# One more block of the up projection with seven products for eight, and other places for the plain units

## The chip, the cores and the metric

The kernel runs on one core of a Trainium2 chip. The metric is the device time of one execution in microseconds. The kernel before takes 1564.11 us (median of three runs, 1563.72 to 1564.22).

## What is computed

One encoder block on 256 tokens (SEQ) of width 2048 (D_MODEL), all in float32: a retention branch and an attention branch, merged by gates, and then an MLP with squared ReLU. The change touches the MLP alone:

```python
z = _rmsnorm(h, norm_mlp_g[l]) @ w_up[l]          # (256, 2048) @ (2048, 8192)
h = h + jnp.square(jax.nn.relu(z)) @ w_down[l]    # (256, 8192) @ (8192, 2048)
return _rmsnorm(h, norm_f_g)
```

## The kernel before

**Number format.** Every float32 operand is split in two parts of the type fp32r: `hi` is the rounded value, made by a cast on ScalarE, and `lo` is the rest, made by a subtraction on VectorE (`split`, L548 to L551). A product is then three matmuls: hi by hi, hi by lo, lo by hi. So each weight tile costs a cast, a subtraction and three passes of TensorE, and VectorE and ScalarE work on weights throughout.

**Two ways through the up projection.** The 8192 columns of `w_up` are computed in two ways.

- A *unit* (`class Unit`, L1264) computes 128 columns for all 256 tokens, with the weights standing in TensorE. It has two parts, one for each half of the depth 2048. A part loads 512 KB, makes one split of 128x1024, and runs eight matmuls of 512 columns (`t_pass1`, L176) and eight of 256 (`t_pass2`, L180). After the second part `evict` (L1288) copies the bank on ScalarE (L1291), adds its halves on VectorE (L1292), and two parts later ScalarE does relu (L1295) and square (L1256), and GpSimd's queue stores the result to a buffer `hid` in HBM (L1257).
- A *block* computes 1024 columns in eight *steps* (`class Step`, L287; `SJ` is 8), with the seven-product form of a 2x2 matrix product: combinations of the operands are made first, then seven products stand for eight. A step covers 256 of the depth and 1024 columns. Its weights come in two loads of 512 KB (`sraw`, L300, and `raw`, L301). VectorE makes the weight forms (L307 for `fa`, L316 and L317 for `fb`). The step has four parts: part 0 takes the raw tile `ra` and makes two products, part 1 takes `fa` and makes two, part 2 takes `fb` and makes two, part 3 takes the remaining raw half-tile and makes one. Each product is three matmuls (L333 to L335). The seven products gather over the eight steps in seven PSUM banks: 3, 4, 2 and 5 in the pool `pmm`, 6, 1 and 7 in the pool `pat`, which has four banks. Units and turns use `pat` too, and so share its last bank while a block runs.

After a block's last part `s_end` (L515) combines the seven banks: four copies on ScalarE and four operations on VectorE at once, and three more on VectorE some parts later (`SUMS`). The result lies with tokens on partitions, and four *turns* (L1302) transpose it on TensorE, four transposes of 128x128 each (L1309), into a bank of `pat`; ScalarE applies relu (L1261) and square and the result is stored. The turns of a block run in part 1 of steps 1 to 4 of the next block, ahead of that part's products; those of the last block run behind the last two units.

**Operand combinations.** The activation side of a block needs combinations too (`Combos`, `combine`, L221 to L245): eight pairs, made two at a time. Two of the four groups are made while the first block runs, started by part number (`MAKE`: at parts 7 and 24) and advanced at even part numbers, four stages of VectorE and ScalarE work each. They borrow two of the five `raw` buffers.

**The order of work.** `stream` (L470) goes through a list `parts`, in which the order is written out: for each part n it issues the loads up to six parts ahead, the splits up to `AHEAD` = 4 parts ahead, and then the matmuls of part n with whatever hangs on it (an eviction, a block's end, a turn). All engines keep this program order. So an eviction of part n stands in ScalarE's and VectorE's queues ahead of the splits of part n + 5.

**How the list is built** (L1331 to L1354). The first three units come ahead (first halves, then second halves), the last two at the end. Before the change `SU` is 3: three blocks compute 3072 columns, and the other 5120 columns are 40 units. Of these, 35 stand between the parts of the steps: one after part 3 of every step but the last of all (23), and twelve more after part 1 of steps 0, 2, 4 and 6 of each block. Behind the last unit the down projection follows in the same list, starting with the hidden pairs that the units made and ending with those of the blocks (`order`, which begins at `ST // 2`).

Of the kernel before, what the change touches and what calls it, by code (L numbers as in the profile page):

```python
# [27 lines left out]
CHUNK = 64  # L28
DFF = 8192
FT = DFF // P  # L30
SU = 3
SJ = KT // 2
ST = SU * 1024 // P
EARLY, LATE = 3, 2
AHEAD = 4
PAIRED = 6
MAKE = 7, 2 * EARLY + 18
SUMS = (4, 7, 10), (0, 1, 2)
MANUAL = {getattr(mybir.EngineType, n) for n in ('Activation', 'DVE', 'PE', 'SP', 'Pool')}
# [66 lines left out]
def block_kernel(ctx: ExitStack, tc: tile.TileContext, A):  # L106
# [1195 lines left out]
    def turn(u, jj):  # L1302
        pT = atps(f"zt{u}{jj}")
        for j in range(2):
            kt = 2 * jj + j
            for t in range(2):
                o = j * S + t * P
                src = zo[:, 0, 2 * t + kt // 4, kt % 4 * P : kt % 4 * P + P]
                PE.transpose(pT[:, o : o + P], src, ident)  # L1309
        square(4 * u + jj, pT)  # L1310

    def step(u, j, qs):
        def end():
            sums = s_end(qs, zo[:, 0].rearrange("p (t c) n -> p t c n", t=2), zo[:, 1])
            next(sums)
            later.extend([d, lambda: next(sums)] for d in SUMS[u == SU - 1])
            turns.extend(lambda jj=jj: turn(u, jj) for jj in range(4))
# [13 lines left out]
    early = [Unit(i, 0) for i in range(EARLY)]  # L1331
    parts = [(e, h) for h in range(2) for e in early]
    units = list(range(EARLY, FT - ST - LATE))
    slots = [(u, j, h) for u in range(SU) for j in range(SJ) for h in (1, 3)][:-1]
    whole = [t for t in slots if t[2] == 3]
    room = len(units) - len(whole)
    halves = [t for t in slots if t[2] == 1]
    if room >= 0:
        use = set(whole) | {halves[i * len(halves) // room] for i in range(room)}
    else:  # L1340
        use = {t for t in whole if t[1] != PAIRED or t[0] >= -room}
    for u in range(SU):
        qs = {}
        for j in range(SJ):
# [69 lines left out]
    def finish(half, t, c, n, lo=0, hi=512):  # L1414
        h = residual(half, t, c)[:, lo:hi]
        ps = both[half].q[ROLE[t, c]][:, lo:hi]
        V.scalar_tensor_tensor(h, in0=ps, scalar=rh2[:, t : t + 1], in1=h, op0=ALU.mult, op1=ALU.add)

        def square():
            SC.activation(ps, h, AF.Square, accum_out=ssf[:, t, n : n + 1])  # L1420

        return square
# [90 lines left out]
    with tc.manual_schedule(engines=MANUAL):  # L1513
        stream(parts, after)
        assert not later
        for t in range(2):
            for c in range(2):
# [10 lines left out]
                else:  # L1528
                    halves = [finish(1, t, 1, 3, 0, 256)]
# [86 lines left out]
```

## Time and profile before

| what | us |
|---|---|
| median of three runs | 1564.11 |
| the profiled execution | 1564.87 |
| its span, first to last instruction | 1563.1 |
| busy: TensorE matmul / weight load | 1550.3 / 1310.8 |
| busy: VectorE / ScalarE / GpSimd | 1317.3 / 962.8 / 39.1 |
| up projection, first unit to first matmul of the down projection | 344.48 |

PE stands for TensorE's matmuls, PEld for its weight loads, DVE for VectorE, ACT for ScalarE, POOL for GpSimd and SP for the engine that issues the weight loads. A row of a timeline begins with the start in us from the start of the span and the duration in us; then come engine, line, operation, output and input, shape, and the count of like instructions in a row; a bracket tells the idle time ahead of it and what ended it. Matmul durations overlap, so that the cost of one is the distance between starts. A row of the waits is: who waited for whom, us in total, times, longest. Names are those of the tiles in the code without their numbers: `zs` is a block's bank, `z` a unit's, `zt` a turn's, `zo` the combined result of a block, `hs` a result on its way to `hid`, `hc` and `hT` the operands, `dn` the down projection's bank.

### The profile page before, as it was taken

Reading aid. Unit: us, or ns where it says so; the run is one execution under the profiler, and the core shown is the slowest. Engines: PE = TensorE matmul, PEld = TensorE weight load, DVE = VectorE, ACT = ScalarE, POOL = GpSimd, SP = SyncE. Lnnn points to the kernel's source line nnn. Section 1 sums busy time; section 2 is a strip of 40 time slices with the busy share of each in tenths; the row PEclk is TensorE's granted clock in tenths of the full one; section 3 lists DMA queues with packets and bytes.
Section 4 is the critical chain, followed back from the end, with each engine's and each line's share of the span. In section 5 each row is a group of like instructions: output and inputs, shape, how many; then the busy total and the mean of one; then the engine's idle time right before and its main releaser. Section 6 shows DMA issues by size and latency. Waiting matters only on the chain.

```text
span 1563.1 us, 21388 instructions
## 1 busy us (share of the span) xinstructions
PE 1550.3 (99%) x7655; PEld 1310.8 (84%) x7655; DVE 1317.3 (84%) x1787; ACT 962.8 (62%) x1416; POOL 39.1 (3%) x76
## 2 busy tenths in 40 slices
PE   9999999999999999999999999999999999999997
PEld 7888888888898888888888888888888888888886
DVE  7998877899977988976566698887978899989996
ACT  7546555566545667874445566676767766656664
POOL 0000000000000000000000000000000100000000
PEclk9999999999999999999999999999999999999999
DMA  8666755466656664445556657676675977686773
GB/s 328 208 202 208 234 163 160 154 202 211 203 170 222 207 197 149 158 127 164 191 197 217 234 193 252 210 229 229 212 247 190 375 269 240 235 308 210 265 256 115
DMA packets 107626, 333.70 MB, mean 213 GB/s; under 512 B 11264, under 2 KB 12160, under 8 KB 106496
## 3 DMA queue, kind: packets, MB, share of 16 engines
q1 hardware_dynamic: 104208, 318.71, 61.3%
q0 software_dynamic: 3168, 11.54, 1.8%
q10 hardware_dynamic: 144, 2.10, 0.4%
q8 instruction: 60, 0.98, 0.2%
q14 instruction: 46, 0.38, 0.1%
HBM read 319.72 MB, written 12.58 MB: 213 GB/s over the span
## 4 chain that ended last, share of the span: by engine, by line
PE 78%; DVE 2%; issue 1%; ACT 1%; DMA 0%; DVEq 0%; POOLq 0%; POOL 0%; ACTq 0%
PE z L176 9%; PE dn L359 7%; PE dn L358 7%; PE dn L357 7%; PE z L180 5%; PE zs L335 2%; PE zs L333 2%; PE zs L334 2%; PE mo L214 2%; PE mo L215 2%; PE mo L217 2%; PE wo L214 2%; PE wo L215 2%; PE wo L217 2%; PE gm L357 2%; PE yr L358 2%
## 5 line engine op out<-in xcount | busy, mean ns | idle before, releaser
L169 DVE TENSOR_TENSOR lo<-raw,hi 128x1024 fp32r<-128x1024 f32 (+1 forms) x148 | 173.2, 1172 | 90.9 <-ACT hi L168 90.8
L551 DVE TENSOR_TENSOR lo<-raw,hi 128x1024 fp32r<-128x1024 f32 (+3 forms) x214 | 232.1, 1101 | 20.1 <-ACT hi L550 19.6
L168 ACT CAST hi<-raw 128x1024 fp32r<-128x1024 f32 (+1 forms) x148 | 149.6, 1012 | 156.0 <-PE mo L215 44.9
L550 ACT CAST hi<-raw 128x1024 fp32r<-128x1024 f32 (+3 forms) x214 | 199.9, 953 | 51.6 <-issue 7.9
L551 DVE TENSOR_TENSOR morelo<-raw,morehi 128x1024 fp32r<-128x1024 f32 (+1 forms) x118 | 127.1, 1098 | 19.0 <-ACT morehi L550 18.5
L550 ACT CAST morehi<-raw 128x1024 fp32r<-128x1024 f32 (+1 forms) x118 | 109.1, 949 | 10.7 <-PE dn L359 2.9
L550 ACT CAST hi<-forms 128x1024 fp32r<-128x1024 f32 x70 | 73.7, 1052 | 51.8 <-DVE forms L307 26.3
L176 PE MATMUL z<-hT,morehi 128*128 128x512 f32 x408 | 101.6, 391 | 0.0
L357 PE MATMUL dn<-hi,dd 128*128 128x512 f32 x230 | 89.6, 389 | 0.0
L359 PE MATMUL dn<-hi,dd 128*128 128x512 f32 x230 | 89.5, 389 | 0.0
L358 PE MATMUL dn<-lo,dd 128*128 128x512 f32 x230 | 89.5, 389 | 0.0
L551 DVE TENSOR_TENSOR lo<-forms,hi 128x1024 fp32r<-128x1024 f32 x70 | 85.0, 1220 | 5.3 <-ACT hi L550 4.9
L176 PEld LDWEIGHTS z<-hT,morehi 128*128 128x128 f32 x408 | 74.9, 188 | 14.4
L1291 ACT COPY hs<-z 128x512 f32<-128x512 f32 x40 | 23.5, 587 | 70.6 <-PE z L180 70.6
L357 PE MATMUL dn<-morehi,dd 128*128 128x512 f32 x156 | 60.7, 389 | 0.0
L358 PE MATMUL dn<-morelo,dd 128*128 128x512 f32 x156 | 60.7, 389 | 0.0
L359 PE MATMUL dn<-morehi,dd 128*128 128x512 f32 x156 | 60.7, 389 | 0.0
L180 PEld LDWEIGHTS z<-hT,morelo 128*128 128x128 f32 x408 | 55.6, 190 | 4.0
L176 PE MATMUL z<-hT,hi 128*128 128x512 f32 x232 | 57.9, 392 | 0.0
L307 DVE TENSOR_TENSOR forms<-raw,sraw 128x1024 f32<-128x1024 f32 x46 | 56.1, 1219 | 1.1 <-DMA raw<-w_up_s 1.1
L180 PE MATMUL z<-hT,morelo 128*128 128x256 f32 x408 | 56.9, 282 | 0.0
L358 PEld LDWEIGHTS dn<-lo,dd 128*128 128x128 f32 x230 | 43.2, 188 | 9.0
(500 smaller groups left out, 4195.1 us busy)
## 6 DMA issues: line engine op xcount, KB each, us to landing
raw<-w_down SPq DMA_DIRECT2D x106, 512.0 KB, 6.1
raw<-w_up SPq DMA_DIRECT2D x80, 512.0 KB, 4.9
raw<-w_rv SPq DMA_DIRECT2D x32, 512.0 KB, 4.9
raw<-w_rg SPq DMA_DIRECT2D x32, 512.0 KB, 4.0
raw<-w_gret SPq DMA_DIRECT2D x32, 512.0 KB, 4.4
raw<-w_ret_o SPq DMA_DIRECT2D x32, 512.0 KB, 5.0
raw<-w_gmla SPq DMA_DIRECT2D x32, 512.0 KB, 4.3
raw<-w_mla_o SPq DMA_DIRECT2D x32, 512.0 KB, 3.7
```

The lines of the kernel that those rows point to most:

```text
L168: SC.copy(hi, raw)
L169: V.tensor_tensor(out=lo, in0=raw, in1=hi.bitcast(F32), op=ALU.subtract)
L176: PE.matmul(out, w[0][:, k], x.both(k0 + k), start=start and k == 0, stop=False)
L180: PE.matmul(out[:, :S], w[1][:, k], x.hi(k0 + k), start=False, stop=stop and k == n - 1)
L214: PE.matmul(out, x.hi(k0 + k, ts), w[0][:, k], start=start and k == 0, stop=False)
L215: PE.matmul(out, x.lo(k0 + k, ts), w[0][:, k], start=False, stop=False)
L217: PE.matmul(out, x.hi(k0 + k, ts), w[1][:, k], start=False, stop=stop and k == nk - 1)
L357: PE.matmul(q, ah, wh, start=start, stop=False)
L358: PE.matmul(q, ah, wl, start=False, stop=False)
L359: PE.matmul(q, al, wh, start=False, stop=self.left[f] == 0)
L550: SC.copy(hi, val)
L551: V.tensor_tensor(out=lo, in0=val, in1=hi.bitcast(F32), op=ALU.subtract)
```

## The change

`SU` becomes 4: four blocks compute 4096 columns, 32 units the other 4096. With three units ahead and two at the end, 27 stand among the steps. Their places are written down anew: one after part 1 of each step but steps 0 and 4 of a block (`WHOLE`), and one after part 3 of a block's last step, between that block and the next. `PAIRED` and the general rule go. The weights are laid out to match, since `_s_steps` and `_t_units` take their columns by `SU`, and `ST`, the count of 128-column groups in blocks, goes from 24 to 32, so that the hidden pairs of the units are 16 to 31 and those of the blocks 0 to 15.

```diff
-SU = 3
+SU = 4
...
-PAIRED = 6
+WHOLE = 0, 4
...
     units = list(range(EARLY, FT - ST - LATE))
-    slots = [(u, j, h) for u in range(SU) for j in range(SJ) for h in (1, 3)][:-1]
-    whole = [t for t in slots if t[2] == 3]
-    room = len(units) - len(whole)
-    halves = [t for t in slots if t[2] == 1]
-    if room >= 0:
-        use = set(whole) | {halves[i * len(halves) // room] for i in range(room)}
-    else:
-        use = {t for t in whole if t[1] != PAIRED or t[0] >= -room}
+    use = {(u, j, 1) for u in range(SU) for j in range(SJ) if j not in WHOLE} | {(u, SJ - 1, 3) for u in range(SU - 1)}
     for u in range(SU):
```

`MAKE`, `SUMS`, `AHEAD`, the first three units and the last two stay as they are.

## The prediction

> **What bounds the kernel now.** I read the page first, then the table of busy time by stretches, the waits of the up-projection stage, and the timelines of single steps in it. The columns of the table are length, busy time (instructions) of PE, PEld, DVE, ACT and POOL, granted clock, DMA share and GB/s. Its first row is the whole up projection (first unit matmul to first matmul of the down projection), then two pairs of steps, then the down projection.
>
> ```profile
> span 1563.1 us, 21388 instructions
> PE 1550.3 (99%) x7655; PEld 1310.8 (84%) x7655; DVE 1317.3 (84%) x1787; ACT 962.8 (62%) x1416; POOL 39.1 (3%) x76
> ```
> ```profile
> 876.13:1220.61 344.48, 344.41 (x1841) 296.85 (x1840) 290.75 (x332) 236.12 (x338) 26.12 (x48) 1.00 0.67 225
> 962.62:988.90 26.28, 26.28 (x140) 22.63 (x139) 21.31 (x24) 16.69 (x23) 1.62 (x3) 1.00 0.63 216
> 1015.18:1042.43 27.25, 27.25 (x149) 23.43 (x147) 22.46 (x26) 18.82 (x27) 2.70 (x5) 1.00 0.68 227
> 1220.61:1520.00 299.39, 299.39 (x1324) 247.89 (x1323) 285.87 (x345) 193.44 (x246) 3.22 (x6) 1.00 0.78 270
> ```
> ```profile
> PEld zs L335 <- DVE lo L551: 0.5, 1, 0.5
> DVE hs L1292 <- ACT hs L1291: 26.7, 19, 2.8
> ```
> TensorE is full, at a granted clock of 1.00, and in the whole up projection it waits once, 0.5 us, for a split on VectorE. So the stage lasts as long as its matmuls, and 344.48 us is their sum. But VectorE is busy 290.75 of these 344.48 us (84%), and it cannot use all of the rest: the queue is in order, and 26.7 us go into standing at a unit's eviction until ScalarE has copied the bank.
>
> What TensorE pays for a step and for a unit stands in its timeline:
>
> ```profile
> 909.68 0.40 PE L333 MATMUL zs<-hi,hT 128*128 128x512 f32 x1
> ...
> 914.47 1.98 PE L176 MATMUL z<-hT,morehi 128*128 128x512 f32 x8
> ...
> 920.03 0.40 PE L333 MATMUL zs<-morehi,hT 128*128 128x512 f32 x1
> ```
> Durations overlap, so I take starts. A step (21 matmuls) is 914.47 - 909.68 = 4.79 us, 0.228 per matmul: its parts 0, 1, 2 have six (1.37 us), part 3 has three (0.68). A unit is 920.03 - 914.47 = 5.56. As a check, two steps and three units are 26.26, and the row has 26.28. The pair with two turns in it is 27.25, so a turn is 0.97 / 2 = 0.485.
>
> VectorE's side of a step, of a block's end and of a unit's eviction:
>
> ```profile
> 1035.96 1.22 DVE L307 TENSOR_TENSOR forms<-raw,sraw 128x1024 f32<-128x1024 f32 x1
> 1037.10 1.22 DVE L551 TENSOR_TENSOR lo<-sraw,hi 128x1024 fp32r<-128x1024 f32 x1
> 1038.24 0.68 DVE L316 TENSOR_TENSOR forms<-forms,sraw 128x512 f32<-128x512 f32 x1
> 1038.95 0.69 DVE L317 TENSOR_TENSOR forms<-forms,raw 128x512 f32<-128x512 f32 x1
> 1039.56 2.42 DVE L551 TENSOR_TENSOR lo<-forms,hi 128x1024 fp32r<-128x1024 f32 x2
> 1041.90 0.69 DVE L551 TENSOR_TENSOR lo<-raw,hi 128x512 fp32r<-128x512 f32 x1
> ```
> ```profile
> 997.69 2.14 DVE L520 TENSOR_TENSOR zo<-zs,zo 128x512 f32<-128x512 f32 x3
> 999.74 0.68 DVE L520 TENSOR_TENSOR zo<-zo 128x512 f32<-128x512 f32 x1
> 1000.34 1.22 DVE L551 TENSOR_TENSOR lo<-raw,hi 128x1024 fp32r<-128x1024 f32 x1
> ```
> ```profile
> 894.60 0.42 DVE L1292 TENSOR_TENSOR hs<-hs 128x256 f32<-128x256 f32 x1
> ```
> By starts again: part 0 of a step is 3.60 us (1.14 + 1.14 + 0.71 + 0.61), parts 1 and 2 are 1.17 each, part 3 is 0.60 (the spacing of the 128x512 rows at 999.74 and 1000.34). **A step is 6.54 us on VectorE against 4.79 on TensorE.** A unit is two splits of 1.14 and 0.34 for its add: 2.62 against 5.56. The units are what lets VectorE keep up. A block's end is 2.65 at once and three more of 0.60 later: 4.45.
>
> **What the change removes and adds.** Eight units go and a block of eight steps comes. The count is what the words say: 64 - 32 - 5 = 27 units stand among the steps, and 6 x 4 + 3 = 27. On TensorE that is -8 x 5.56 + 8 x 4.79 + 4 turns x 0.485 = **-4.2 us**, and the old wait of 0.5 has no reason to return in its place: -0.5. On VectorE it is 8 x 6.54 + 4.45 - 8 x 2.62 = +35.8: busy 326.6 in a stage whose matmuls now need 340.3, 96%. So on average it still fits, and the question is where it does not fit locally. The bytes stay the same (a step and a unit both load 1 MB), and ScalarE stays below VectorE. The down projection takes its hidden pairs in another order, but the same shapes and positions; I cost it at nothing, covered by stores that are many steps old; a pair that came late would show as a wait for its load.
>
> *Block 0.* Before, a unit follows step 0's part 1 and another its part 3; now step 0 has none, and the first unit stands in step 1. Besides its steps VectorE makes two groups of operand combinations there, placed by part number (parts 8 to 14 and 24 to 30), and this place does not move, so the second one now falls onto step 3's unit and step 4, which has no unit:
>
> ```profile
> L231 DVE TENSOR_TENSOR raw<-hT x2: 1218/1218/1219, 900.4 to 933.1; 128x1024 f32<-128x1024 f32 x2
> L237 DVE TENSOR_TENSOR raw<-raw x2: 418/418/419, 906.8 to 936.5; 128x256 f32<-128x256 f32 x2
> L238 DVE TENSOR_TENSOR raw<-raw x2: 418/419/420, 907.2 to 936.8; 128x256 f32<-128x256 f32 x2
> L240 DVE TENSOR_TENSOR raw<-raw,raw x2: 418/418/418, 909.8 to 939.2; 128x256 f32<-128x256 f32 x2
> L241 DVE TENSOR_TENSOR raw<-raw,raw x2: 425/426/426, 910.2 to 939.7; 128x256 f32<-128x256 f32 x2
> L551 DVE TENSOR_TENSOR hc<-raw,hc x2: 1216/1216/1216, 912.6 to 946.0; 128x1024 fp32r<-128x1024 f32 x2
> ```
> ```profile
> 893.75 0.40 PE L333 MATMUL zs<-morehi,hT 128*128 128x512 f32 x1
> ```
> A group is 4.13 us of durations, 3.65 less 0.08 of overlap each. From the last early unit's add (894.60 + 0.34 = 894.94, a time that the change leaves alone) VectorE has, up to the split that part 1 of step 5 needs: four steps 26.16, three units 7.86, parts 0 and 1 of step 5 4.77, the combinations without the last split 3.65 + 2.51. That is 44.95 us, done at 939.9 if it never waits. TensorE starts step 0 at 893.75, step 1 at 898.54, and wants that split 4 steps, 3 units, one part and two matmuls later: 898.54 + 19.16 + 16.68 + 1.37 + 0.46 = 936.2. VectorE is 3.7 us late, and about 0.3 for signals and weight loads that show: **+4.0** (my bounds are 3 and 6). The upper bound is for a load that comes late:
>
> ```profile
> raw<-w_up_s SPq DMA_DIRECT2D x23, 512.0 KB, 4.4
> ```
> Step 2's second load goes out when the split of step 1's unit frees its buffer, at 894.94 + 3.60 + 1.17 + 1.14 = 900.9, and lands at about 905.3; VectorE gets to it at 905.6 (a step, two unit splits and 1.8 of combinations after 894.94). Two us later would be two us more. After step 5 every step has its unit, and per step and unit VectorE needs 9.16 of 10.35, so it recovers.
>
> *Between blocks.* A block ends: unit of step 7, its parts 2 and 3, one unit, then step 0 and parts 0 and 1 of step 1 without any unit. Splits are issued four parts ahead, behind the unit's eviction in the queue. At the end of step 7's unit (call it 0) the queue has nothing further done than the next unit's splits. The add ends at about 1.15 (0.15 for the signal, estimated; copy and add). Then VectorE does step 0 6.54, the block's end 2.65, the next unit's add 0.34, and parts 0 and 1 of step 1 3.60 + 1.17: done at 15.45. TensorE wants it at 2.05 + 5.56 + 4.79 + 1.37 + 0.485 + 0.46 = 14.71. With 0.15 for the signal: 0.9 late.
>
> The second wait there is new in kind. Each turn (one in part 1 of steps 1 to 4 of the next block) writes a bank of a pool of four, of which three hold products 6, 1 and 7; the unit right behind part 1 needs the same last bank, and has to wait until ScalarE's relu has read the turn. ScalarE's rows:
>
> ```profile
> 1026.22 0.59 ACT L1291 COPY hs<-z 128x512 f32<-128x512 f32 x1 [2.65 <-PE z L180]
> 1026.71 1.05 ACT L550 CAST hi<-forms 128x1024 fp32r<-128x1024 f32 x1
> 1027.65 0.62 ACT L550 CAST morehi<-raw 128x512 fp32r<-128x512 f32 x1
> 1028.17 0.60 ACT L1261 ACTIVATE hs<-zt 128x512 f32<-128x512 f32 x1
> 1028.81 0.63 ACT L1256 ACTIVATE hs<-hs 128x512 f32<-128x512 f32 x1
> 1029.35 0.40 ACT L1295 ACTIVATE hs<-hs 128x256 f32<-128x256 f32 x1
> 1029.78 0.42 ACT L1256 ACTIVATE hs<-hs 128x256 f32<-128x256 f32 x1
> 1030.10 1.03 ACT L550 CAST morehi<-raw 128x1024 fp32r<-128x1024 f32 x1
> ```
> By starts: a big cast 0.94, a small one 0.52, the relu of a turn 0.60, the last two operations of a unit 0.75. This is a turn with a unit behind it, and only two casts lie between the copy and the relu; the pair of 27.25 us shows no wait. In the new order the queue holds more. In step 1 the forms are ready at 11.82 (1.15 + 6.54 + 2.65 + 0.34 + 1.14), then come a cast, a unit's end, three casts, a small cast and the relu: 0.94 + 0.75 + 2.82 + 0.52 + 0.60 = 5.63, with the signal 17.6; TensorE is there at 14.25 + 1.37 + 0.9 = 16.5: 1.1 to 1.2 more. In steps 2 and 3, from the end of the unit before: 0.15 + 0.49 + two casts 1.88 + 0.75 + 0.94 + 0.52 + 0.60 + 0.15 = 5.5 against 2.05 + 1.37 + 0.485 + 1.37 = 5.27: 0.25 each (bounds 0 and 0.6). Together 0.9 + 1.2 + 0.5 = 2.6 at each of three boundaries: **+7.8** (bounds 4 and 11).
>
> The Trainium skill (Perfetto Trace Analysis, the section on matmuls under tensor performance) advises that independent matmul groups rotate through different PSUM banks, so that one group's evacuation runs beside the next one's matmuls. That speaks against the new places; taken alone it would price the nine pairs of turn and unit at a whole evacuation each, 9 x 0.60 = 5.4 us, where the queue's order gives 3 x 1.7 = 5.1. The pair of 27.25 us, in which the bank is shared too, shows that sharing alone costs nothing.
>
> At step 4, where a turn but no unit stands, the same sums leave 0.9 us of slack (the split of step 5's part 1 at 8.25 after the unit of step 3, wanted at 9.15), so I cost it at nothing in blocks 1 to 3. If VectorE still lagged there, its lag would show.
>
> **Sum.** -4.2 - 0.5 + 4.0 + 7.8 = +7.1 us. The profiled execution took 1564.87 (span 1563.1 and 1.8 around it, which stays), so it would be 1572.0; the median of the runs, 1564.11, is 0.76 below that one, so I forecast **1571.2 us**. A check from the other side: VectorE's 326.6 us and its old 26.7 us at evictions are 353.3 for the stage, +8.8.
>
> **Rivals.** *All of it is covered* (the other side). The down projection runs VectorE at 285.87 of 299.39 us (95%) without a TensorE wait. If the up stage did so at 96%, only -4.7 would be left: 1559.4. Its place is the start of a block; it decides if step 1's forms are done by about 9.7 instead of 11.8 after the last unit, earlier by both waits (0.9 and 1.2), which brings the relu forward as well. Against it: the down parts are even, while a unit's eviction holds back the queue here. [...] I give 0.12.
>
> *Only VectorE's lag counts*, and the bank is handed back in time: -4.7 + 4.0 + 2.7 = +2.0, 1566.1, no measurable change. For it: the waits in steps 2 and 3 are within the error of the sum; against it: the 1.2 us in step 1 is not. 0.18.
>
> *VectorE never recovers*: if it also keeps a wait of 1.4 us (26.7 / 19) at each of 32 evictions, the stage is 326.6 + 44.8 = 371.4, +26.9, 1591.0. Against it: waiting for a copy is what a late queue stops doing. 0.08.
>
> **How the numbers follow.** The forecast itself has 0.62, with a range of its own of 1566.4 to 1576.4 (the two sums at their bounds are 7 to 17, against -4.7, on 1564.11). Two runs of this kernel can be told apart at about 0.2%, 3.1 us. Faster by more than that is only the first rival, 0.12; within it, the second, 0.18; slower, the forecast and the last, 0.70. The range of 1563.5 to 1578 leaves out the first and the last rival.
>
> **What would show it.** In the changed profile the stage should take about 351.5 us instead of 344.48, DVE about 327 busy in it. TensorE should wait for lo in steps 2 and 5 of block 0, and near the end of part 1 of step 1 of blocks 1, 2 and 3; z should wait for the relu of the turn (L1261) behind it. Per pair of step and unit elsewhere 10.35, with a turn 10.84 to 11.1. I am wrong if the stage is under 345 us, if TensorE's waits are for DMA, or if the down projection's 299.39 us move by more than 1.

## The result, and the profile after

The change takes 1571.62 us (median of four runs, 1571.23 to 1572.55), the kernel before 1564.16 beside it (1563.72 to 1564.43): 1.0049 times as long, 95% interval 1.0031 to 1.0066. It is slower by 7.5 us, more than the 0.2% that a measurement can tell. A later repeat (e11) gave 1571.65 against 1564.58, ratio 1.0046 (1.0033 to 1.0059). The profiled execution took 1572.55 us, where the prediction's sum gave 1572.0 for it. Its page begins:

```profile
span 1570.8 us, 21306 instructions
PE 1551.3 (99%) x7583; PEld 1303.9 (83%) x7583; DVE 1349.0 (86%) x1826; ACT 970.2 (62%) x1420; POOL 37.0 (2%) x72
```

72 matmuls fewer, and yet a longer span. The busy table by stretches, with the columns as in the prediction, shows where: the whole up projection, one pair of step and unit inside a block, and the same 1324 matmuls of the down projection as before.

```profile
876.58:1228.30 351.72, 344.63 (x1770) 289.30 (x1768) 322.70 (x371) 243.40 (x342) 23.98 (x44) 1.00 0.66 220
1033.76:1044.11 10.35, 10.35 (x55) 8.86 (x53) 9.31 (x11) 6.68 (x10) 0.54 (x1) 1.00 0.67 212
1228.30:1527.69 299.39, 299.39 (x1324) 247.90 (x1323) 285.77 (x345) 193.39 (x246) 3.24 (x6) 1.00 0.77 270
```

The stage went from 344.48 to 351.72, +7.24; the down projection is the same to the hundredth; a pair inside a block costs 10.35 as before, and the clock is 1.00 in all three. So the loss lies in the stage and at certain places in it. The waits of the stage, for weight loads and then for VectorE's evictions:

```profile
PEld z L176 <- ACT hs L1261: 6.8, 9, 1.3
PEld zs L335 <- DVE morelo L551: 4.7, 4, 2.0
PEld zs L335 <- DVE lo L551: 3.4, 5, 0.9
```
```profile
DVE hs L1292 <- ACT hs L1291: 15.1, 14, 2.6
```

Before, TensorE had one wait of 0.5 here. Now it has nine for the relu of a turn and nine for a split. The timeline of the weight loads tells where (the bracket is the idle time of the loads; some of it hides behind matmuls under way):

```profile
911.81 0.19 PEld L335 LDWEIGHTS zs<-lo,hc 128*128 128x128 f32 x1 [0.92 <-DVE lo L551]
...
937.25 0.19 PEld L335 LDWEIGHTS zs<-morelo,hT 128*128 128x128 f32 x1 [1.47 <-DVE morelo L551]
...
940.50 0.19 PEld L335 LDWEIGHTS zs<-morelo,hc 128*128 128x128 f32 x1 [2.03 <-DVE morelo L551]
...
985.38 1.69 PEld L176 LDWEIGHTS z<-hT,hi 128*128 128x128 f32 x8 [1.34 <-ACT hs L1261]
...
996.54 1.67 PEld L176 LDWEIGHTS z<-hT,hi 128*128 128x128 f32 x8 [0.47 <-ACT hs L1261]
```

The first three lie in block 0, in part 1 of step 2 and in parts 0 and 1 of step 5. The other two stand at the first boundary: the unit behind part 1 of step 1 of block 1, and the unit of step 2. A like one follows in step 3 (0.45), and two waits for splits, 0.42 and 0.80, come ahead of them in step 1; all five come again at the two later boundaries.

What they cost is read from the starts of the matmuls:

```profile
928.76 0.40 PE L333 MATMUL zs<-morehi,hc 128*128 128x512 f32 x1
...
941.54 0.63 PE L176 MATMUL z<-hT,morehi 128*128 128x512 f32 x2
...
980.44 0.39 PE L334 MATMUL zs<-hi,hT 128*128 128x512 f32 x1
...
981.16 0.40 PE L333 MATMUL zs<-hi,hc 128*128 128x512 f32 x1
...
982.52 0.40 PE L334 MATMUL zs<-hi,hc 128*128 128x512 f32 x1
983.28 0.50 PE L335 MATMUL zs<-lo,hc 128*128 128x512 f32 x1 [0.36 <-DVE lo L551]
983.62 0.39 PE L333 MATMUL zs<-hi,hc 128*128 128x512 f32 x1
...
984.09 0.40 PE L335 MATMUL zs<-lo,hc 128*128 128x512 f32 x1
985.39 2.12 PE L176 MATMUL z<-hT,hi 128*128 128x512 f32 x8 [0.91 <-ACT hs L1261]
```

From 928.76 to 941.54 stand 42 matmuls of steps (parts 2 and 3 of step 3, step 4, parts 0 and 1 of step 5): 12.78 us for 42 x 0.228 = 9.58. That is 3.20 lost; 0.78 more is lost at 911.81, where the 21 matmuls between two units take 5.57 for 4.79. Block 0 loses **3.98**. At the boundary a matmul of a step follows the one before by 0.228 where nothing waits. From 980.44 to 981.16 it is two in 0.72, 0.26 lost; from 982.52 to 983.62 two in 1.10, 0.64 lost: **0.9** for the two splits. From 984.09 to the unit's first it is 1.30, 1.07 lost, and a unit behind such a wait takes 5.67 to 5.71 for 5.56: **1.2** for the bank in step 1. In steps 2 and 3 the unit's first comes 0.42 after the matmul before it, 0.19 lost, and with the slower unit it is 0.31 and 0.33. A boundary loses 2.75, the three **8.3**. Together that is 12.3. In e10 below, where TensorE waits nowhere, the same number of matmuls makes a stage of 339.42, and 351.72 is 12.30 more.

### The profile page after: what moved, and what is told of

Same layout as the page of the kernel before. It is cut to its first block, busy times and chain, and to the rows that moved or that the text cites. A ratio compares the mean times of both kernels' runs of the same rounds, so it can differ in the third digit from the quotient of the medians.

```text
span 1570.8 us, 21306 instructions
## 1 busy us (share of the span) xinstructions
PE 1551.3 (99%) x7583; PEld 1303.9 (83%) x7583; DVE 1349.0 (86%) x1826; ACT 970.2 (62%) x1420; POOL 37.0 (2%) x72
## 4 chain that ended last, share of the span: by engine, by line
PE 73%; DVE 4%; ACT 2%; issue 2%; DMA 0%; DVEq 0%; POOLq 0%; POOL 0%; ACTq 0%
PE dn L358 7%; PE dn L359 7%; PE dn L357 7%; PE z L176 6%; PE z L180 3%; PE zs L335 2%; PE zs L333 2%; PE zs L334 2%; PE mo L214 2%; PE mo L215 2%; PE mo L217 2%; PE wo L217 2%; PE wo L214 2%; PE wo L215 2%; PE gm L359 2%; PE gm L357 2%
## 5 line engine op out<-in xcount | busy, mean ns | idle before, releaser
L551 DVE TENSOR_TENSOR lo<-raw,hi 128x1024 fp32r<-128x1024 f32 (+3 forms) x236 | 251.6, 1082 | 26.6 <-ACT hi L550 25.6
L550 ACT CAST hi<-raw 128x1024 fp32r<-128x1024 f32 (+3 forms) x236 | 217.1, 938 | 57.4 <-issue 9.4
L551 DVE TENSOR_TENSOR morelo<-raw,morehi 128x1024 fp32r<-128x1024 f32 (+1 forms) x88 | 93.8, 1084 | 2.9 <-ACT morehi L550 2.8
L550 ACT CAST morehi<-raw 128x1024 fp32r<-128x1024 f32 (+1 forms) x88 | 81.1, 941 | 7.0 <-issue 2.1
L550 ACT CAST morehi<-forms 128x1024 fp32r<-128x1024 f32 x51 | 53.6, 1050 | 44.9 <-DVE forms L307 26.2
L551 DVE TENSOR_TENSOR lo<-forms,hi 128x1024 fp32r<-128x1024 f32 x57 | 69.5, 1220 | 3.2 <-ACT hi L550 2.5
L176 PEld LDWEIGHTS z<-hT,hi 128*128 128x128 f32 x288 | 52.3, 188 | 14.4 <-ACT hs L1261 4.5
L551 DVE TENSOR_TENSOR morelo<-forms,morehi 128x1024 fp32r<-128x1024 f32 x51 | 62.2, 1219 | 2.2 <-ACT morehi L550 1.7
L176 PE MATMUL z<-hT,morehi 128*128 128x512 f32 x224 | 56.2, 393 | 0.9 <-ACT hs L1261 0.9
L357 PEld LDWEIGHTS dn<-hi,dd 128*128 128x128 f32 x240 | 45.0, 188 | 9.4
```

Of the source, the lines that this page charges most:

```text
L176: PE.matmul(out, w[0][:, k], x.both(k0 + k), start=start and k == 0, stop=False)
L357: PE.matmul(q, ah, wh, start=start, stop=False)
L550: SC.copy(hi, val)
L551: V.tensor_tensor(out=lo, in0=val, in1=hi.bitcast(F32), op=ALU.subtract)
```

## The experiments

The theory was the prediction's: the order costs three separate sums. VectorE is behind in block 0, through the early steps without units and the combinations; it is behind again where a block's end meets steps without units; and ScalarE's queue gives a turn's bank back late. The main rival was that the fourth block itself is too much, wherever its units stand. Every length called "stage" runs from the first unit matmul to the first matmul of the down projection in the profiled execution. The times of each kernel before beside the experiments are 1564.4 (e1 to e4), 1564.6 (e5 to e8), 1564.6 (e9 to e11) and 1564.6 (e12).

**e1: is it the turn's bank?** The turn moves from part 1 of the step, right ahead of the unit, to part 3, behind it.

```diff
-            if part == 1:
+            if part == 3:
                 self.between()
```

> The changed kernel, but each turn stands ahead of part 3 of its step instead of part 1, so that 3.4 us of matmuls lie between a turn and the next unit. Theory (the unit behind a turn waits for the one free bank of the pool, 9 waits, 1.2 us in step 1 and 0.25 in steps 2 and 3, after ScalarE's relu in its queue): the nine waits for L1261 vanish; without the turn's 0.485 us ahead of it, part 1 of step 1 waits somewhat longer for VectorE, 1.4 instead of 0.9; a boundary loses 1.4 instead of 2.6 us, so 3.6 less in all: 1568.0 us. Rival (VectorE is the bound, and the bank's wait only covers what VectorE would cost anyway): the waits move to VectorE's lo, and the time stays at 1571 to 1572.

Measured 1568.39 us, ratio 1.0024 (1.0015 to 1.0033), stage 347.96: 3.8 of the 7.2 us come back. Its waits in the stage:

```profile
PEld zs L335 <- DVE morelo L551: 5.3, 4, 2.0
PEld zs L335 <- DVE lo L551: 4.2, 5, 1.2
PEld zt L1309 <- ACT hs L1291: 0.7, 3, 0.2
```

The relu's nine waits are gone, and the waits for splits are a little longer, since TensorE now comes to them earlier. The bank's share is real and separable.

**e2: is it where the combinations fall?** The second group starts eight parts earlier.

```diff
-MAKE = 7, 2 * EARLY + 18
+MAKE = 7, 2 * EARLY + 10
```

> The changed kernel with the second group of operand combinations begun at part 16 instead of part 24, that is beside steps 2 and 3 of block 0 and no longer beside step 4, which has no unit. Theory (VectorE's queue from 894.9 us on has 45 us of work up to part 1 of step 5, wherever the combinations stand in it): block 0 still loses 4.0 us, spread otherwise, 1571.6 us within 1. Rival (the loss comes from the combinations falling onto the step without a unit): block 0 loses 1.5 us, 1569.

Measured 1572.83, ratio 1.0053 (1.0041 to 1.0066), stage 352.84. The waits of block 0 now come in six pieces instead of three, in part earlier. So it is not the place of the group that counts but its amount of work: VectorE has no pause in this stretch into which it could be moved.

**e3: do the splits come too late?** While blocks run, the splits of a part are issued five parts ahead in place of four, so that VectorE's spare time inside a block is used ahead of the boundary.

```diff
-    def stream(parts, after):
+    def stream(parts, after, deep=0):
...
-            while prepped < min(len(parts), n + ahead + 1):
+            while prepped < min(len(parts), n + ahead + 1 + (0 < n < deep)):
...
     assert not units
+    deep = len(parts)
...
-        stream(parts, after)
+        stream(parts, after, deep)
```

> The changed kernel with the splits of the up projection issued five parts ahead instead of four; nothing else moves. Theory (at a block's end VectorE's queue stands idle behind the eviction of step 7's unit, with nothing issued beyond the next unit's splits): part 0 of the next block's first step gets done in that idle time, VectorE is then 2 to 3 us early at step 1, the wait for lo there (0.9 us) and the relu's lateness in step 1 (1.2) go, the 0.25 in steps 2 and 3 stay, block 0 loses about 0.7 less: 1564.6 us. Rival (VectorE has too much to do over the stage as a whole): look-ahead makes no work less, at most 2 us come back, 1569.6 or more.

Measured 1567.16, ratio 1.0016 (1.0007 to 1.0025), stage 347.03: 4.7 us come back, less than expected.

```profile
PEld z L176 <- ACT hs L1261: 5.9, 9, 1.6
PEld zs L335 <- DVE morelo L551: 3.3, 3, 1.6
PEld zs L335 <- DVE lo L551: 0.2, 1, 0.2
```

No boundary has a wait for a split any more, and those of block 0 fell from 4.4 (0.92 + 1.47 + 2.03) to 3.5; but the bank's waits stay. I had taken it that the earlier forms would bring the relu forward. They do, but one more split is issued ahead of it, and so one more cast stands in ScalarE's queue before it.

**e4 and e5: is it the places, or the fourth block?** e4 is four blocks under the old rule for the units (one after part 3 of every step but step 6); e5, set up when the result of e4 was known, leaves out step 3 in place of 6. Both bring back the lines of the old rule that the diff removes, with

```diff
-WHOLE = 0, 4
+PAIRED = 6
```

in e4 and `PAIRED = 3` in e5.

> Four blocks, but the units in the places of the rule of before: after part 3 of every step except step 6 (and the last). So the block count alone, without the new places. Theory (the places make the waits, not the count): no wait for L1261, since two parts lie between a turn and the next unit; block 0 loses nearly nothing, since its steps 0 to 5 all have a unit; at each boundary the block's end is late in VectorE's queue, behind the splits of steps 6 and 7, and product 4 of the next block waits about 1.2 us for its bank: -4.7 + 3.7, 1563 us (1560 to 1566). Rival (with four blocks VectorE is 96% busy, and that costs wherever the units stand): 1569 or more.

> Four blocks with the units after part 3 of every step except step 3 (and the last): the kernel with the old places, but the pair of steps without a unit between them moved from 6 and 7, at the block's end, to 3 and 4. Theory (a block's end must not meet a late VectorE): a unit now stands after step 6, so that step 7 starts with its splits done; the waits at the three boundaries (0.6 us for lo in step 0, 1.1 us of the turn for the unit's copy, 0.5 for the bank of product 4) go, 4 to 5 us; block 0 keeps the 2.4 us in step 2 that a late load cost (raw of step 2 came 1.5 us after VectorE was ready for it), plus 0.6 where the second group of combinations falls onto steps 3 and 4: 1563 us (1561 to 1565). Rival (VectorE at 96% costs some 3 us over matmuls wherever the gap is): 1568 or more, as with the old places.

Measured: e4 1568.94, ratio 1.0027 (1.0017 to 1.0038), stage 347.53; e5 1568.45, ratio 1.0027 (1.0017 to 1.0038), stage 348.51. Both expectations failed. The waits of e4, TensorE's and then one of VectorE's:

```profile
PEld zs L335 <- DVE morelo L551: 5.0, 5, 2.4
PEld zt L1309 <- ACT hs L1291: 3.4, 3, 1.1
```
```profile
DVE forms L307 <- DMA raw<-w_up_s: 1.5, 1, 1.5
```

The relu's waits are absent, as expected, and at the boundaries a turn waits for a unit's copy instead. In e5, where they were expected to vanish, these shrink to 1.3 us in three waits. But block 0 loses time under each of the three orders: by the starts of its matmuls 3.98 us in the change, 3.2 in e4 (weight loads wait 2.38 and 1.13) and 8.3 in e5 (1.91, 2.15, 0.91 and 2.38). In e4 and e5 loads of `raw` arrive late as well (waits of 1.5 and 2.9 us); that this is because the combinations hold two of the five buffers is the reading that e7 tests. So the rival has a part of the truth. With the places of before, too, the fourth block would have cost more than it saves, 3.1 us by the stage and 4.5 by the medians; the change's own places cost another 3 to 4.

Of e5's 8.3 us, 1.6 are no wait. Behind the wait of 2.38 eight matmuls of steps start 0.43 apart instead of 0.228, from 948.31 to 951.71, and the granted clock of this stretch is 0.50. In e7 below the same happens behind waits of 1.31 and 1.94, from 955.43 to 958.83, again at 0.50. Why the clock falls there, and not behind the waits of the change, no run here shows.

**e6: both repairs.** e1 and e3 together, on the change's places.

> The changed kernel with both: turns ahead of part 3 of their steps, and splits of the up projection five parts ahead. Theory (bank wait and eviction wait are separate terms and add up): the boundaries lose nothing any more, block 0 its 3.3 us as with the deeper look-ahead alone, 1563 us (1562 to 1564.5). Rival (both cures free the same time): no better than the better of the two, 1567.

Measured 1562.95, ratio 0.9991 (0.9982 to 1.0), stage 342.68. All the boundaries are clean but for one 0.5 us wait of a turn; what stays is block 0's 3.5 us of waits. Each repair alone gave 3.2 to 4.5 us of run time, both give 8.7: with the turn behind the unit, the cast that e3 puts ahead of the relu no longer holds up a weight load.

**e7: e5 with the combinations later.**

```diff
-MAKE = 7, 2 * EARLY + 18
+MAKE = 11, 2 * EARLY + 26
```

> As the kernel with the pair of steps at 3 and 4, and the two groups of operand combinations begun at parts 11 and 32 instead of 7 and 24, so that the load of step 2 goes out before the first group takes two of the five raw buffers, and the second group stands behind the pair of steps. Theory: the 2.4 us in step 2 and the 0.6 at steps 3 and 4 go, and some 1 us stays: 1560.5 us (1559.4, all covered, to 1562). Rival (block 0's loss is VectorE's work, not the load): as without the move, 1563.

Measured 1566.33, ratio 1.0012 (1.0003 to 1.0021), stage 346.59. It is 2.1 us below e5 and far above the 1562 at most that the theory gave, and above its rival too.

```profile
PEld zs L335 <- DVE lo L551: 2.0, 2, 1.2
PEld zs L334 <- DVE hc L551: 1.9, 1, 1.9
PEld zs L333 <- ACT hc L550: 1.3, 1, 1.3
```

No load is late now, which fits the buffers as the reason for that. But the products wait for the combinations themselves (`hc`), which are needed by their own step, and 1.6 us go with the lower clock. Made earlier, the combinations make the splits late; made later, they are late themselves.

**e8 and e10: is that all?** The two late groups of combinations are left out of the change (e8) and of e6 (e10).

```diff
-MAKE = 7, 2 * EARLY + 18
+MAKE = ()
...
-            o = self.t[j // 4][:, j % 4]
+            o = self.t[0][:, j % 4]
```

> The changed kernel without the two groups of operand combinations in block 0: the products of steps 4 to 7 of each block use the combinations of steps 0 to 3 instead, so that part of the computation is left out; every matmul, load and split of weights stays. Theory (VectorE's queue up to part 1 of step 5 decides block 0): 6.2 us less of VectorE's work make it 2.5 us early instead of 3.7 late, block 0 loses nothing, the boundaries keep their 8: 4.0 less, 1567.6 us. Rival (steps 0 and 4 without units starve TensorE by themselves): 2 us or more of the loss stay, 1569.6 or more.

> The kernel with turns ahead of part 3 and splits five parts ahead, without the two groups of operand combinations (the products of steps 4 to 7 use those of steps 0 to 3, so that part of the computation is left out). Theory (three terms, block 0, VectorE's lag and the bank at the boundaries, are all of the loss): nothing is left of it, and the matmuls alone decide: 4.7 us below the kernel before, 1559.6 on the scale of 1564.4. Rival (something else costs too): 1561 or more.

Measured: e8 1567.83, ratio 1.0021 (1.0013 to 1.003), stage 347.63; e10 1559.89, ratio 0.997 (0.9958 to 0.9982), stage 339.42. In e8 the waits are those of the boundaries alone:

```profile
PEld z L176 <- ACT hs L1261: 6.8, 9, 1.3
PEld zs L335 <- DVE lo L551: 2.4, 4, 0.8
PEld zs L335 <- DVE morelo L551: 1.2, 2, 0.8
```

The 6.8 for the relu is the figure of the change; the two others are (0.42 + 0.80) x 3. So block 0 loses its 4.1 us only with the combinations, the steps without units do not starve TensorE by themselves, and the two places do not act on each other. In e10 TensorE waits nowhere in the stage: the three terms are the whole of the loss.

**e9: the combinations on GpSimd**, which is idle 98% of the time, in e6.

```diff
-        V.tensor_tensor(out=a2, in0=a11, in1=a12, op=ALU.subtract)
+        E.tensor_tensor(out=a2, in0=a11, in1=a12, op=ALU.subtract)
...
-            return combine(self.pair, 2 * c, self.t[-1][:, c % 2 * 2 : c % 2 * 2 + 2])
+            return combine(self.pair, 2 * c, self.t[-1][:, c % 2 * 2 : c % 2 * 2 + 2], E=G if c > 1 else V)
```

> The kernel with turns ahead of part 3 and splits five parts ahead, and besides the additions and subtractions of the two groups of operand combinations in block 0 on GpSimd, which is busy 2% of the time; their splits stay on ScalarE and VectorE. Theory (what is left of the loss, 3.3 us in block 0, is VectorE's 45 us of work up to step 5): VectorE sheds 5.0 us there, no wait for lo stays in block 0: 1559.7 us (1559 to 1560.5). Rival (GpSimd's operations, whose length no run here has shown, come too late for the splits behind them, or slow VectorE): the splits wait in order, 1563 or more.

Measured 1567.17, ratio 1.0016 (1.0007 to 1.0025), stage 346.95, 4.3 more than e6. The rival held; its lines are in the last section.

**e12: a unit where block 0 lacks one.** e6, with the one unit that the last block can spare given to step 4 of block 0.

```diff
-WHOLE = 0, 4
+WHOLE = (0,), (0, 4), (0, 4), (0, 4, 6)
...
-if j not in WHOLE
+if j not in WHOLE[u]
```

> The kernel with turns ahead of part 3 and splits five parts ahead, and one unit moved: step 4 of block 0 gets one, step 6 of block 3 loses its own (both after part 1). Theory (the rest of the loss is VectorE's queue up to step 5 of block 0, 3.3 us): the unit gives TensorE 5.56 us there for 2.62 of VectorE's, 2.9 us of slack, and block 3, where VectorE has caught up and no combinations are made, has room for a second pair of steps without a unit: block 0 loses 0.4, block 3 nothing to 1, so 1560.5 us (1559.5 to 1561.5) against 1564.4 before. Rival (the unit taken away is missed where it stood): the loss moves to block 3, 1563.

Measured 1560.16, ratio 0.9973 (0.9962 to 0.9983), its stage and its waits (columns as above):

```profile
875.45:1215.19 339.74, 339.74 (x1769) 290.46 (x1768) 322.28 (x371) 243.32 (x342) 24.04 (x44) 1.00 0.68 228
```
```profile
PEld zs L335 <- DVE lo L551: 0.5, 2, 0.3
PEld zt L1309 <- ACT hs L1291: 0.2, 1, 0.2
```

339.74 is what the prediction's sum for the matmuls alone gives, 344.48 - 4.2 - 0.5 = 339.8; that it is so close is partly chance, since e10 has 339.42 without any wait. Of block 0's waits 0.5 us at two weight loads is left, though the combinations are made as before: what is lost there takes both, the combinations and a step without a unit. And nothing is lost in block 3 where the unit was taken away. The kernel does all the work of the change, with four blocks, and is 4.4 us faster than the kernel before and 11.5 faster than the change. The fourth block's saving is there; three decisions about order had spent it.

## Why the prediction was right, step by step

**The matmuls, -4.2, and the old wait, -0.5.** Right within 0.4: they give a stage of 339.8, and e10 without any wait has 339.42. Steps and units cost 4.79 and 5.56 as costed; a turn costs 0.46 (it and six matmuls of a step take 1.83 from 1016.80 on) for the 0.485 costed.

**Block 0, +4.0.** Measured 3.98, and the mechanism can be followed in VectorE's timeline: from the first of these rows to the last it works without a pause, but for 0.2 us behind the first.

```profile
895.36 1.22 DVE L307 TENSOR_TENSOR forms<-raw,sraw 128x1024 f32<-128x1024 f32 x1
...
939.23 1.22 DVE L551 TENSOR_TENSOR morelo<-forms,morehi 128x1024 fp32r<-128x1024 f32 x1
```

The stage began 0.45 us later than before (876.58 for 876.13), so the last row's end at 940.45 is 940.0 on the old scale; the prediction said 939.9. Its load of 905.3 did not come late. The 0.3 for signals and weight loads is of the size seen: a load begins 0.05 after the end of the split it waited for (940.45 and 940.50), and behind each of the three waits the next matmul starts 0.33 or 0.34 later instead of 0.228. One reason given on the way was wrong: that the second group of combinations hurts because it falls onto step 4. e2 moved it away and gained nothing. It is the amount, 6.2 us of combinations up to part 1 of step 5, in a queue that is full; e8 without it has no wait there.

**Boundaries, 3 x 2.6 = +7.8.** Measured 3 x 2.75 = 8.3, and each part by itself: the splits 0.9 predicted, 0.9 measured; the bank in step 1 1.2 predicted, 1.2 measured; in steps 2 and 3 0.25 each predicted, 0.31 and 0.33 measured. The prediction's other price for the bank, a whole evacuation of 0.60 at each of the nine turns, comes out near the same total (5.4 predicted, 5.5 measured) by chance: the nine are not alike, and their sizes are those of the queue. The 0.15 for a signal was an estimate; here the copy of a unit starts at 975.62, 0.20 after the first matmul behind that unit. The order of ScalarE's queue is as worked out:

```profile
979.66 1.06 ACT L550 CAST hi<-forms 128x1024 fp32r<-128x1024 f32 x1 [2.50 <-DVE forms L307]
980.63 0.41 ACT L1295 ACTIVATE hs<-hs 128x256 f32<-128x256 f32 x1
981.07 0.42 ACT L1256 ACTIVATE hs<-hs 128x256 f32<-128x256 f32 x1
981.39 1.98 ACT L550 CAST hi<-raw 128x1024 fp32r<-128x1024 f32 x2
983.27 1.05 ACT L550 CAST morehi<-forms 128x1024 fp32r<-128x1024 f32 x1
984.23 0.61 ACT L550 CAST morehi<-raw 128x512 fp32r<-128x512 f32 x1
984.74 0.59 ACT L1261 ACTIVATE hs<-zt 128x512 f32<-128x512 f32 x1
```

ScalarE stands idle for 2.50 us until VectorE has made the forms, and then 5.1 us of casts and the unit's end go ahead of a relu that takes 0.6; it ends at 985.33, and the unit's loads go on at 985.38. So this wait for ScalarE is VectorE's lateness handed on: the engine named in the wait was itself waiting.

**Sum and time.** +7.1 predicted, +7.24 measured in the stage and +7.5 by the medians. That the stage is so near is in part luck: the matmuls came out 0.4 lower and the boundaries 0.5 higher than costed.

**What was off.** VectorE's busy time: 326.6 predicted, 322.7 measured. The durations of all VectorE operations in the stage, count times mean, rose by 36.7 us (309.2 to 345.9), near the 35.8 costed; but busy time counts overlapping stretches once, and a VectorE operation that follows directly on another overlaps it by 0.08 (1.14 from start to start, 1.22 long). With more operations and fewer pauses the overlaps grew from 18.5 to 23.2 us. Nothing in the sum used this number but the check from the other side, 326.6 + 26.7 = 353.3: that came near 351.72 by luck, as its other term was 15.1 and not 26.7.

**The rivals.** *All of it covered* fell, though e12 shows that it needs no more than another order. It named the earlier forms as the point from which it decides, both waits at once; e3 made the splits early and lost the boundary's waits for them, but not the relu's. *Only VectorE's lag counts* fell with the nine waits for the relu, which e1 took away for 3.2 us. *VectorE never recovers* fell with the waits at evictions, which shrank from 26.7 to 15.1 in place of staying. What I had not weighed is that the fourth block has a price under the old order too (e4).

## What to carry to other kernels

Where engines with queues in order feed each other, sum the work of a queue between two points and compare it with when its result is wanted; shares of busy time (VectorE 92%, TensorE 98% here) cannot tell that 12 us will be lost, nor where. A wait is mended in the queue that is named only if that engine was working: here the relu was late because of what stood ahead of it, and moving the turn two parts on, or issuing splits one part earlier, each undid one sum; both together undid those of the boundaries, and block 0 needed a unit in step 4 besides. When a change that saves work comes out slower, check whether the saving is there first; if it is, as in e12, the order is what to change.

## What the runs showed of the hardware that was not expected

In e9 VectorE was slower beside GpSimd. First GpSimd's rows (the first is an addition that takes VectorE 1.22 us), then VectorE's from the same time on:

```profile
899.77 2.79 POOL L231 TENSOR_TENSOR raw<-hT 128x1024 f32<-128x1024 f32 x1
902.64 1.60 POOL L237 TENSOR_TENSOR raw<-raw 128x256 f32<-128x256 f32 x1
904.20 1.72 POOL L238 TENSOR_TENSOR raw<-raw 128x256 f32<-128x256 f32 x1
905.88 1.18 POOL L240 TENSOR_TENSOR raw<-raw,raw 128x256 f32<-128x256 f32 x1
```
```profile
899.08 4.57 DVE L551 TENSOR_TENSOR morelo<-raw,morehi 128x1024 fp32r<-128x1024 f32 x2
903.57 1.75 DVE L551 TENSOR_TENSOR lo<-forms,hi 128x1024 fp32r<-128x1024 f32 x1
905.25 1.22 DVE L551 TENSOR_TENSOR lo<-raw,hi 128x512 fp32r<-128x512 f32 x1
906.39 1.75 DVE L307 TENSOR_TENSOR forms<-raw,sraw 128x1024 f32<-128x1024 f32 x1
...
911.07 1.22 DVE L551 TENSOR_TENSOR lo<-forms,hi 128x1024 fp32r<-128x1024 f32 x1
```

While GpSimd computes, a 128x1024 operation of VectorE takes 1.75 us and up to 3.43 (the second of the two at 899.08, which starts 1.14 later), and 1.22 again once GpSimd is done. GpSimd's 128x256 operations take 0.74 to 1.72 against 0.42 on VectorE; what they would take alone no run shows. The Trainium skill (SBUF — State Buffer, the section on the two separate sides) says that a VectorE operation with two inputs in SBUF and a GpSimd operation that reads SBUF exclude each other for a whole instruction. These rows agree, and their ends show it. GpSimd's four operations end at 902.56, 904.24, 905.92 and 907.06, and VectorE's at 903.65, 905.32, 906.47 and 908.14: a 128x1024 operation ends 1.08 or 1.09 after GpSimd's, the 128x512 one 0.55. That is an operation that does its whole work once GpSimd has finished, not one that goes on more slowly beside it. It holds for all ten GpSimd operations of block 0, each of which lengthens one VectorE operation (the three 128x512 ones end 0.54 to 0.56 behind). In one case, at 938.11, VectorE's row begins 0.35 before GpSimd's, so which of the two has the port first cannot be read from the starts of the rows. Worked out from the rows, the ten cost VectorE 9.1 us, where it was spared 5.0; its busy time in the stage is 326.5 us for e6's 322.4, and so e9 lost against e6.
